# Sums of squares by TensorE for the second norm, and five gate/up tiles with two products ahead of the main loop

## The chip, the cores and the metric

The kernel runs on one NeuronCore of a Trainium2 chip. The metric is the device time of one execution in microseconds; the time of a kernel is the median of its runs. The engines are TensorE (PE in the profile, with its weight loads as PEld), VectorE (DVE), ScalarE (ACT), GpSimd (POOL), and SyncE (SP), which here only issues transfers.

## What is computed

Two layers of an encoder trunk over 1,040 positions (16 learned ones and 1,024 of the input), with 1,024 features. Each layer is a mixer and a feed-forward part, each behind an RMSNorm and added to the residual; the change lies at the second norm of each layer:

```python
def rmsnorm(x, w):
    xf = x.astype(jnp.float32)
    y = xf * lax.rsqrt(jnp.mean(xf * xf, axis=-1, keepdims=True) + RMS_EPS)
    return (y * w.astype(jnp.float32)).astype(x.dtype)

def swiglu(h, w_gate_up, w_down):
    gate, up = jnp.split(h @ w_gate_up.astype(h.dtype), 2, axis=-1)
    return (jax.nn.silu(gate) * up) @ w_down.astype(h.dtype)
...
    for l in range(DEPTH):
        h = h + hybrid_mixer(rmsnorm(h, norm1_w[l]), ..., w_out[l])
        h = h + swiglu(rmsnorm(h, norm2_w[l]), w_gate_up[l], w_down[l])
```

The mixer is a delta-rule head group beside a gated convolution, joined by one output projection `w_out`. Everything is float32; the feed-forward has 2,816 inner features, so 22 tiles of 128.

## The kernel before

**Layout.** Features lie on the 128 partitions, positions along the row: the residual `hr` is eight tiles of 128 x 1040. A sum of squares over features is therefore a sum over eight tiles and then over partitions. In the second layer the feed-forward leaves out the 16 learned positions (`o0 = 16`), so its rows have 1,024 columns.

**Products.** A float32 product is made of three passes in the fast fp32r form: both operands are split into a high part (`hi`, by a copy on ACT) and the rest (`lo`, by a subtraction on POOL or DVE), and PE adds hi*hi, hi*lo and lo*hi in one bank (`dense`, L145 to L172; `prod`, L1055). The splitting of a weight block of 128 x 512 is `wsplit` (L129, L130) for the projections and `w_op` (L1042, L1043) for gate and up.

**The feed-forward's scheme.** Gate and up together are one product, done by a Strassen-Winograd scheme with seven products per tile in place of eight. Its left operands are the weight blocks A11, A12, A22 and sums S1 to S4 of blocks; its right operands are parts and sums of the scaled residual: B11, B21, B22 and T1 to T4, each 128 x 4 x `NB` as a hi and a lo part. `NB` is half a row: 520 columns in layer 0, 512 in layer 1. The halves are made of quarters of the row: half 0 is the two middle quarters, half 1 the two outer ones (`half`, L932). In layer 0 a product is made in two pieces of 260 columns (`NJ` = 2), in layer 1 in one of 512. B11 and B21 need half 0 alone.

**Order of the work around the change.**

1. `out_part(z, m)` (L941) adds to half `z` of residual tile `m` the part of the output projection that comes from the delta-rule heads: `dense` with DVE's `add_h` (L905) as evacuation, in two column chunks, then the square on ACT, the running sum of squares in `ss` on DVE or POOL, and a store of the tile to `hd`. It runs over `m` for z = 0, then for z = 1.
2. Between the parts, DVE and ACT build the T operands: `t_split_w` (L177 and L176, a scaled split), scalings of the other half in place (L1001, which must wait until the store to `hd` has read the tile), sums (`t_sum`, L977), and `t_split` (L964 on ACT, L965 on DVE).
3. The early tiles: for the first `NE` = 4 of 22 tiles the two products that need only half 0, A11*B11 and A12*B21, are done here, ahead of the main loop (L1083 to L1098). Their results wait in the rows `u` and `g`; ACT copies them out (L1095, L1098).
4. `finish_bc` (L200) closes the sum: four matmuls with a block of ones, each on a quarter of the columns and into 32 partitions of its own of one bank, so that all positions lie as 4 x 32 partitions by 260 (256) columns; then the root on ACT, the reciprocal on DVE, a store of 4 rows and a broadcast back into `ss`:

```python
        for j in range(4 if sums else 0):
            mm(ps[32 * j:32 * j + 32, 0:e], ones[:, 0:32], ss[:, n0 + e * j:n0 + e * j + e], start=True, stop=True, skip_group_check=True)
        r = c4k("r")[:, 0:e]
        act(out=r, in_=ps[:, 0:e], func=AF.Sqrt, scale=1.0 / D, bias=cols["eps"])
        nc.vector.reciprocal(out=r, in_=r)
```

5. The main loop over 22 tiles (L1256): weight loads on SP's queue, the sums S1 to S4 on DVE (L1266, L1267, L1270, L1271), their splits (`w_op`), five products for the early tiles and seven for the others, with DVE adding the products together (L1289, L1300, L1303, L1307, L1316). Some additions stand between two products that share a bank, so that the second product waits for them. Then gate and up are multiplied by the reciprocal root `ss` (L1330 on POOL, L1331 on DVE), SiLU, the product of both (L1333), and the store to `ad`.
6. Among the main loop's tiles stand eight sums S1 of the down projection's weights (L1146), loaded by SP into `c` buffers.

At the first norm of the kernel the sums of squares are already made by PE: eight sets of four fp32 matmuls of 260 columns (`first_sums`, L252).

**What sets the order.** The program is written in the order of one thread; a scheduler (Tile, with a timeline of its own and the priorities set by `at_prio`) decides where each instruction stands in the queue of its engine. Each queue is then worked off in order. Banks of PSUM come from rings: `acc` has three, `f` and `b` two, `a` one (L69); `pbank` (L1048) deals them out for gate and up. Full rows called `c` (`c4k`, L65) are a ring of two that serves the squares, `r`, the `u` of the last early tile and later the S1 sums. The weight tiles `whi`/`wlo` have three buffers, `raw` two, and the row buffers `ck2` five.

Of the kernel before, what the change touches and what calls it, by code (L numbers as in the profile page):

```python
# [7 lines left out]
F32 = mybir.dt.float32  # L8
F32R = mybir.dt.float32r
BF16 = mybir.dt.bfloat16  # L10
AF = mybir.ActivationFunctionType
# [4 lines left out]
KT = 8  # L16
# [26 lines left out]
def trunk(ctx: ExitStack, tc: tile.TileContext, xT, w_in, w_ba, w_out, w_gu, w_dn,  # L43
# [15 lines left out]
    def row(tag, dt=F32, bufs=1):  # L59
        return sb.tile([128, L], dt, tag=tag, bufs=bufs, name=nm(tag))  # L60
# [4 lines left out]
    def c4k(tag="c"):  # L65
        return sb.tile([128, L], F32, tag="c", bufs=2, name=nm(tag))

    def bank(tag):
        return psp.tile([128, 512], F32, tag=tag, bufs={"acc": 3, "a": 1, "f": 2, "b": 2}[tag], name=nm("p" + tag))  # L69
# [62 lines left out]
    def wload(src, nk):  # L132

        res = []
        step = min(nk, WK)
        for k0 in range(0, nk, step):
            kk = min(step, nk - k0)
            hi = wp.tile([128, WK, 128], F32R, tag="whi", name=nm("whi"))
            lo = wp.tile([128, WK, 128], F32R, tag="wlo", name=nm("wlo"))
            wsplit(src[:, k0:k0 + kk, :], hi[:, 0:kk, :], lo[:, 0:kk, :])  # L140
            for k in range(kk):
                res.append((hi[:, k, :], lo[:, k, :]))
        return res

    def dense(ws, xs, chunks, evac, pool=None):  # L145

        for (n0, n1) in chunks:
            n = n1 - n0
            ps = (pool or pacc)()
            K = len(xs)  # L150
            here = tc.cur_priority
            if mmp[0] is not None:
                at_prio(mmp[0])
            for k in range(K):
                (wh, wl), (xh, xl) = ws[k], xs[k]
                mm(ps[:, :n], wh, xh[:, n0:n1], start=(k == 0), stop=False)  # L156
                mm(ps[:, :n], wh, xl[:, n0:n1], start=False, stop=False)  # L157
                mm(ps[:, :n], wl, xh[:, n0:n1], start=False, stop=(k == K - 1))  # L158
            if mmp[0] is not None:
                mmp[0] = tc.cur_priority  # L160
                at_prio(here)
            here = tc.cur_priority
            if evp[0] is not None:
                at_prio(evp[0])
            evac(ps[:, :n], n0, n1)
            if evp[0] is not None:
                evp[0] = tc.cur_priority
                at_prio(here)
            for q in (jobs, jobs2, jobs3):
                f = q.pop(0) if q else None  # L170
                if f is not None:
                    f()  # L172
# [27 lines left out]
    def finish_bc(ss, n0, n1, dst, ps=None):  # L200

        e = (n1 - n0) // 4
        sums = ps is None
        ps = bank("a") if sums else ps
# [5 lines that stand above are left out]
        dma(dst[:, 0:e], r.rearrange("(a b) c -> a b c", b=32)[:, 0, :])  # L210
        if 4 * e == L:
            dma(ss[:, n0:n1], dst.rearrange("a e -> (a e)").partition_broadcast(128))
        else:
            dma(ss[:, n0:n1].rearrange("p (a e) -> p a e", a=4), dst[:, 0:e].partition_broadcast(128))
# [64 lines left out]
    for l in range(DEPTH):  # L279
# [623 lines left out]
        def add_h(m, then=None):  # L903
            def f(ps, n0, n1):
                tt(out=hr[m][:, n0:n1], in0=ps, in1=hr[m][:, n0:n1], op=ALU.add)  # L905
                if then is not None:
                    then(n0, n1)
            return f
# [23 lines left out]
        def half(ap, z):  # L932

            v = ap.rearrange("p (g e) -> p g e", g=4) if len(ap.shape) == 2 else ap.rearrange("p k (g e) -> p k g e", g=4)
            s = slice(1, 3) if z == 0 else slice(0, 4, 3)
            return v[:, s, :] if len(ap.shape) == 2 else v[:, :, s, :]

        at_prio(base + 3000000)
        ss = row("rstd")

        def out_part(z, m):  # L941
            dense(wload(w_out[l, m, :, 0:4, :], 4), os_, hcut[z], add_h(m), pwide)

            v, sv = half(hr[m][:, o0:L], z), half(ss[:, o0:L], z)
            if m == 0:
                act(out=sv, in_=v, func=AF.Square)
            else:
                sq = c4k("sq")[:, 0:NB].rearrange("p (g e) -> p g e", g=2)
                act(out=sq, in_=v, func=AF.Square)
                (ptt if z == 1 and m % 2 == 0 else tt)(out=sv, in0=sv, in1=sq, op=ALU.add)  # L950
            for (n0, n1) in hcut[z]:
                dma(hd[m][:, n0:n1], hr[m][:, n0:n1])

# [36 lines left out]
        for m in range(KT + 2):  # L990
            if m < KT:
                out_part(1, m)
            if m == 0:
                t_split_w(T["B21"], 7, 0)
            k = m - 2
            if k < 0:
                continue
            if k < 4:
                if k == 0:
                    T["T1"] = t_tile(Y[0][2])  # L1000
                ts(out=hx(k, 1), in0=hx(k, 1), scalar1=pcol(P_N2 + k), scalar2=None, op0=ALU.mult)  # L1001
                t_sum(k, 0, hx(k, 0), npar[:, k:k + 1], hx(k, 1), ALU.add)
                if k % 2:
                    t_split(T["T1"], X0, 0, k - 1)
            else:
                c = pcol(P_N2 + k)
                if k == 4:
                    T["B22"] = t_tile(Y[0][1])
                t_split_w(T["B22"], k, 1)
                t_sum(k - 4, 1, hx(k, 1), c, hx(k - 4, 1))  # L1010
                t_sum(k, 1, hx(k, 1), c, hx(k - 4, 0))
                t_sum(k, 0, hx(k, 0), c, hx(k, 1))
# [67 lines left out]
            return loc(ps, 0)  # L1080


        NE = 4  # L1083
        early = {}
        for f in range(NE):
            A11, A12 = raw4("raw"), raw4("raw")
            dma(A11, w_gu[l, f, 0, :, 0:4, :])
            dma(A12, w_gu[l, f, 0, :, 4:8, :])
            w1, w2 = w_op(A11, True), w_op(A12, True)
            g, u = (row(Y[1], F32, 3), row(X[1], F32, 3)) if f < 3 else (row(Y[1] + "f"), c4k())  # L1090
            early[f] = g, u
            ab = [pbank() for j in range(NJ)]
            for j in range(NJ):
                prod(ab[j], w1, T["B11"], j, True)
                act(out=part(u, 0, j), in_=pin(ab[j]), func=AF.Copy)  # L1095
            for j in range(NJ):
                prod(ab[j], w2, T["B21"], j, False)
                act(out=part(g, 0, j), in_=pin(ab[j]), func=AF.Copy)  # L1098

        finish_bc(ss, o0, L, rsd[0])  # L1100

# [399 lines left out]
```

## Time and profile before

| | |
|---|---|
| time, median of 3 runs | 2607.66 us (2607.26 to 2610.53) |
| the profiled execution's own time | 2614.81 us |
| its span, first to last instruction | 2612.7 us |
| mean granted TensorE clock | 0.984 |
| busy: PE, DVE, ACT, POOL | 96%, 63%, 40%, 42% |

The page and the trace are of one execution, the profiled one. A line such as `L252 PE MATMUL pb<-sq,ones x64` names the line of the kernel, the engine, the operation, the tile written, those read, and how often; forms stand as partitions x columns. A line of the timeline starts with the start in us and the duration; the bracket at its end is the idle time of the engine before it and what ended it. Starts of matmuls follow each other faster than their durations, since they are pipelined. One fp32 matmul of the program is two instructions in the profile.

### The profile page before, as it was taken

What the parts mean: (1) busy time and instruction counts of PE and PEld (TensorE: products, weight loads), DVE (VectorE), ACT (ScalarE), POOL (GpSimd) and SP (SyncE); (2) the same over time, 40 slices, a digit from 0 to 9 for tenths busy, and PEclk for the clock granted to TensorE, in tenths of its full rate; (3) what the DMA queues carried; (4) which work ended last, traced back from release to release, by engine and by line L of the source; (5) the groups of instructions that cost most, each with busy time, mean ns of one, the idle gap of its engine ahead of it and who ended that gap; (6) DMA issues with size and microseconds to landing.
All of it is one profiled execution on the core that took longest, in us unless ns stands there. A gap on an engine that the chain in (4) does not pass through costs nothing.

```text
span 2612.7 us, 45153 instructions
## 1 busy us (share of the span) xinstructions
PE 2508.1 (96%) x17442; PEld 2294.1 (88%) x17442; DVE 1654.4 (63%) x2481; ACT 1045.9 (40%) x1933; POOL 1105.0 (42%) x838
## 2 busy tenths in 40 slices
PE   8999999999999999989999989999989999998997
PEld 6989999898899999989999978998967778886876
DVE  4688433648766666667656874236688777668656
ACT  5664322435233333434445633324452333333444
POOL 2141311225666666645321203122367667665552
PEclk9999999999999999989999999999999999999998
DMA  3458264524422222763324581545333222248431
GB/s 126 135 185 268 90 215 148 176 80 125 135 91 99 94 74 74 252 198 111 97 86 136 186 283 63 182 159 197 116 121 129 94 102 85 79 141 273 133 108 65
DMA packets 213571, 360.03 MB, mean 138 GB/s; under 512 B 25268, under 2 KB 87676, under 8 KB 213356
## 3 DMA queue, kind: packets, MB, share of 16 engines
q1 hardware_dynamic: 180684, 310.69, 36.1%
q10 hardware_dynamic: 30496, 42.09, 5.1%
q0 software_dynamic: 2176, 4.36, 0.6%
q8 instruction: 137, 2.24, 0.4%
q14 instruction: 78, 0.64, 0.1%
HBM read 266.60 MB, written 90.46 MB: 137 GB/s over the span
## 4 chain that ended last, share of the span: by engine, by line
PE 54%; DVE 9%; DMA 4%; issue 3%; POOL 2%; ACT 1%; POOLq 0%; ACTq 0%; DVEq 0%; SPq 0%
PE pacc L156 5%; PE pacc L158 5%; PE pacc L157 5%; PE pacc L1060 3%; PE pacc L1062 3%; PE pacc L1061 3%; PE pb L1060 2%; PE pf L1060 2%; PE pb L1062 2%; PE pb L1061 2%; PE pf L1062 2%; PE pf L1061 2%; PE pacc L1400 1%; PE pacc L1402 1%; PE pacc L1401 1%
## 5 line engine op out<-in xcount | busy, mean ns | idle before, releaser
L130 POOL TENSOR_TENSOR wlo<-raw,whi 128x512 fp32r<-128x512 f32 x132 | 177.0, 1342 | 788.3 <-ACT whi L129 639.4
L156 PE MATMUL pacc<-a,whi 128*128 128x346 f32 (+1 forms) x808 | 265.5, 332 | 10.2 <-ACT whi L129 8.3
L158 PE MATMUL pacc<-a,wlo 128*128 128x346 f32 (+1 forms) x808 | 265.1, 330 | 0.4 <-DVE wlo L130 0.4
L156 PE MATMUL pacc<-b,whi 128*128 128x346 f32 (+2 forms) x672 | 234.8, 350 | 0.0
L158 PE MATMUL pacc<-b,wlo 128*128 128x346 f32 (+2 forms) x672 | 233.2, 348 | 0.0
L157 PE MATMUL pacc<-a,whi 128*128 128x346 f32 (+1 forms) x688 | 227.5, 331 | 2.7 <-DVE a L900 2.5
L129 ACT ACTIVATE whi<-raw 128x512 fp32r<-128x512 f32 x168 | 105.3, 629 | 244.6 <-PE pacc L157 169.3
L157 PE MATMUL pacc<-b,whi 128*128 128x346 f32 (+2 forms) x580 | 200.5, 347 | 0.5 <-DVE b L900 0.5
L156 PEld LDWEIGHTS pacc<-a,whi 128*128 128x128 f32 x808 | 154.5, 192 | 14.5 <-ACT whi L129 10.1
L1043 POOL TENSOR_TENSOR wlo<-rw,whi 128x512 fp32r<-128x512 f32 x92 | 134.8, 1467 | 71.7 <-ACT whi L1042 70.0
L158 PEld LDWEIGHTS pacc<-a,wlo 128*128 128x128 f32 x808 | 154.5, 191 | 2.1 <-issue 0.8
L157 PEld LDWEIGHTS pacc<-a,whi 128*128 128x128 f32 x688 | 132.2, 192 | 7.1 <-issue 2.9
L156 PEld LDWEIGHTS pacc<-b,whi 128*128 128x128 f32 x672 | 127.3, 190 | 11.0 <-issue 3.1
L158 PEld LDWEIGHTS pacc<-b,wlo 128*128 128x128 f32 x672 | 127.3, 190 | 9.2 <-issue 0.8
L1043 POOL TENSOR_TENSOR a<-rw,a 128x512 fp32r<-128x512 f32 x64 | 105.6, 1651 | 69.5 <-ACT a L1042 69.3
L1043 POOL TENSOR_TENSOR b<-rw,b 128x512 fp32r<-128x512 f32 x64 | 92.0, 1439 | 82.3 <-ACT b L1042 49.5
L157 PEld LDWEIGHTS pacc<-b,whi 128*128 128x128 f32 x580 | 109.9, 190 | 7.8 <-DVE b L900 1.0
L1042 ACT ACTIVATE whi<-rw 128x512 fp32r<-128x512 f32 x92 | 57.8, 630 | 146.5 <-DVE rw L1270 84.8
L1266 DVE TENSOR_TENSOR rw<-rw,rw 128x512 f32<-128x512 f32 x44 | 67.4, 1532 | 49.9 <-POOL wlo L1043 34.6
L1271 DVE TENSOR_TENSOR rw<-raw,rw 128x512 f32<-128x512 f32 x44 | 97.4, 2214 | 1.2
L1043 POOL TENSOR_TENSOR wlo<-raw,whi 128x512 fp32r<-128x512 f32 x50 | 76.6, 1533 | 36.5 <-ACT whi L1042 27.9
L1042 ACT ACTIVATE b<-rw 128x512 fp32r<-128x512 f32 x64 | 40.2, 630 | 119.8 <-PE pacc L1061 32.3
(970 smaller groups left out, 8420.2 us busy)
## 6 DMA issues: line engine op xcount, KB each, us to landing
raw<-in_w_in SPq DMA_DIRECT2D x112, 256.0 KB
raw<-in_w_gu SPq DMA_DIRECT2D x104, 256.0 KB
rw<-in_w_gu SPq DMA_DIRECT2D x88, 256.0 KB
rec<-aqd SPq DMA_DIRECT2D x62, 256.0 KB
rec<-vkd SPq DMA_DIRECT2D x61, 256.0 KB
rw<-in_w_dn SPq DMA_DIRECT2D x70, 192.0 KB
raw<-in_w_out SPq DMA_DIRECT2D x48, 256.0 KB
b<-ad SPq DMA_DIRECT2D x45, 260.0 KB
```

The costliest lines, as they stand in the source:

```text
L129: act(out=hi, in_=raw[:, 0:kk, :], func=AF.Copy)
L130: (tt if lov[0] else ptt)(out=lo, in0=raw[:, 0:kk, :], in1=hi.bitcast(F32), op=ALU.subtract)
L156: mm(ps[:, :n], wh, xh[:, n0:n1], start=(k == 0), stop=False)
L157: mm(ps[:, :n], wh, xl[:, n0:n1], start=False, stop=False)
L158: mm(ps[:, :n], wl, xh[:, n0:n1], start=False, stop=(k == K - 1))
L1042: act(out=hi, in_=src, func=AF.Copy)
L1043: ptt(out=lo, in0=src, in1=hi.bitcast(F32), op=ALU.subtract)
L1060: mm(ps[:, :CW], w[0][:, k, :], th[:, cs], start=first and k == 0, stop=False, skip_group_check=True)
L1061: mm(ps[:, :CW], w[0][:, k, :], tl[:, cs], start=False, stop=False, skip_group_check=True)
L1062: mm(ps[:, :CW], w[1][:, k, :], th[:, cs], start=False, stop=stop and k == nk - 1, skip_group_check=True)
L1266: tt(out=s1t, in0=A21, in1=A22, op=ALU.add)
L1271: tt(out=A21, in0=A11, in1=A21, op=ALU.subtract)
```

## The change

The running sum in `ss` goes. In its place each square of 128 x 520 (512) is summed over the partitions by PE: four fp32 matmuls with 32 columns of ones, on quarters of 130 (128) columns, into four strips of 32 partitions of the one bank `a`, which adds up over all eight tiles. Half 0 lies in the left, half 1 in the right part of the bank's first 260 (256) columns. The matmuls of one square are issued behind the next part's `dense` (`sq_sums`). The square of the first tile goes to a `c` buffer like the others. `sq_finish` does the root and the reciprocal, once for both halves, a store of 4 rows, and four broadcast loads that put each strip back to its quarter of the row; it stands in the loop of the second half after its last tile, so ahead of the early tiles. `finish_bc` there goes. The early tiles become five; the fifth keeps its gate in a row of its own and its up in a `c` buffer.

```diff
+        QB = NB // 4
+        sqs = []
+        sps = bank("a")
+
+        def sq_sums():
+            while sqs:
+                sq, z, m = sqs.pop()
+                for j in range(4):
+                    mm(sps[32 * j:32 * j + 32, QB * z:QB * z + QB], ones[:, 0:32], sq[:, QB * j:QB * j + QB], start=(m == 0), stop=(m == KT - 1), skip_group_check=True)
+
+        def sq_finish(dst):
+            sq_sums()
+            r = c4k("r")[:, 0:2 * QB]
+            act(out=r, in_=sps[:, 0:2 * QB], func=AF.Sqrt, scale=1.0 / D, bias=cols["eps"])
+            nc.vector.reciprocal(out=r, in_=r)
+            dma(dst[:, 0:2 * QB], r.rearrange("(a b) c -> a b c", b=32)[:, 0, :])
+            for z in range(2):
+                for i in range(2):
+
+                    q = (1 + i, 3 * i)[z]
+                    dma(ss[:, cut[q]:cut[q + 1]].rearrange("p (a e) -> p a e", a=2), dst[2 * i:2 * i + 2, QB * z:QB * z + QB].partition_broadcast(128))
+
         def out_part(z, m):
             dense(wload(w_out[l, m, :, 0:4, :], 4), os_, hcut[z], add_h(m), pwide)
-
-            v, sv = half(hr[m][:, o0:L], z), half(ss[:, o0:L], z)
-            if m == 0:
-                act(out=sv, in_=v, func=AF.Square)
-            else:
-                sq = c4k("sq")[:, 0:NB].rearrange("p (g e) -> p g e", g=2)
-                act(out=sq, in_=v, func=AF.Square)
-                (ptt if z == 1 and m % 2 == 0 else tt)(out=sv, in0=sv, in1=sq, op=ALU.add)
+            sq_sums()
+
+            sq = c4k("sq")[:, 0:NB]
+            act(out=sq.rearrange("p (g e) -> p g e", g=2), in_=half(hr[m][:, o0:L], z), func=AF.Square)
+            sqs.append((sq, z, m))
             for (n0, n1) in hcut[z]:
                 dma(hd[m][:, n0:n1], hr[m][:, n0:n1])
...
             k = m - 2
+            if m == KT:
+                sq_finish(rsd[0])
...
-        NE = 4
+        NE = 5
         early = {}
         for f in range(NE):
             A11, A12 = raw4("raw"), raw4("raw")
             dma(A11, w_gu[l, f, 0, :, 0:4, :])
             dma(A12, w_gu[l, f, 0, :, 4:8, :])
             w1, w2 = w_op(A11, True), w_op(A12, True)
-            g, u = (row(Y[1], F32, 3), row(X[1], F32, 3)) if f < 3 else (row(Y[1] + "f"), c4k())
+            g, u = (row(Y[1], F32, 3), row(X[1], F32, 3)) if f < 3 else (row((Y, X)[f % 2 == 0][1] + "f"), c4k())
...
-        finish_bc(ss, o0, L, rsd[0])
```

## The prediction

> **What bounds the kernel now.** I read the page's busy shares first, then a table of stretches around the two places of the change, then TensorE's own waits there. A layer's second norm lies between the output projection and the feed-forward's main loop: about 570 to 740 us in layer 0, 1860 to 2020 us in layer 1.
>
> ```profile
> PE 2508.1 (96%) x17442; PEld 2294.1 (88%) x17442; DVE 1654.4 (63%) x2481; ACT 1045.9 (40%) x1933; POOL 1105.0 (42%) x838
> ...
> 590.00:600.00 10.00, 10.00 (x86) 10.00 (x85) 6.92 (x13) 4.70 (x8) 4.87 (x4) 1.00 0.62 175
> 610.00:620.00 10.00, 6.36 (x49) 5.76 (x48) 10.00 (x14) 5.76 (x9) 5.91 (x4) 0.97 0.33 96
> 620.00:630.00 10.00, 8.65 (x53) 8.66 (x54) 10.00 (x12) 6.42 (x12) 4.81 (x5) 0.69 0.39 118
> 1910.00:1920.00 10.00, 8.87 (x31) 6.44 (x31) 10.00 (x11) 5.97 (x10) 6.89 (x4) 0.85 0.39 125
> 1980.00:2000.00 20.00, 15.87 (x60) 11.95 (x59) 17.17 (x16) 4.92 (x8) 16.38 (x9) 0.91 0.41 134
> 2150.00:2200.00 50.00, 50.00 (x217) 40.52 (x216) 36.26 (x32) 15.96 (x26) 32.91 (x20) 1.00 0.28 101
> ```
>
> A stretch's columns are its length, then busy us and count of PE, weight loads, DVE, ACT and POOL, then the granted TensorE clock. PE is 96% busy: matrix work added in a stretch like 590 to 600 lengthens the run one for one, while an instruction taken from DVE or POOL there is worth nothing. From 610 to 630 it is the other way round: DVE has no idle time, PE has 5 us of it and runs part of the rest at a reduced clock. What PE waits for there, by engine, awaited instruction, us in total, times, longest, first in layer 0 (594 to 742 us), then in layer 1 (1896 to 2020 us):
>
> ```profile
> PE pacc L1060 <- DVE a L905: 2.5, 1, 2.5
> PE pa L1060 <- DVE b L1303: 2.1, 1, 2.1
> PE pacc L1060 <- DVE a L1289: 1.8, 2, 1.3
> PE pf L1060 <- DVE a L905: 1.4, 1, 1.4
> PE pf L1060 <- DVE c L1307: 1.4, 1, 1.4
> PE pb L1060 <- DVE a L1307: 1.3, 1, 1.3
> PE pacc L1060 <- DVE a L1307: 1.3, 1, 1.3
> PE pb L1060 <- ACT whi L1042: 1.0, 1, 1.0
> ...
> PE pf L1060 <- DVE b L905: 2.7, 1, 2.7
> PE pa L1060 <- DVE a L1303: 2.4, 1, 2.4
> PE pf L1060 <- DVE b L1307: 2.0, 1, 2.0
> PE pa L206 <- DVE rstd L950: 1.4, 1, 1.4
> PE pa L1060 <- DVE c L1289: 1.2, 1, 1.2
> PE pb L1062 <- POOL wlo L1043: 1.2, 1, 1.2
> PE pf L1060 <- ACT b L1095: 1.0, 1, 1.0
> PE pb L1060 <- ACT b L1042: 0.9, 1, 0.9
> PE pf L156 <- DVE b L905: 0.7, 1, 0.7
> ```
>
> The waits fall in two groups. L905 is DVE's add of an output chunk to the residual: PE wants the bank back and DVE is behind. L1289, L1303 and L1307 are DVE's additions of products in the main loop's first tiles. The change can win only these waits and the slow clock; everything it adds to PE outside them is paid.
>
> **The price of the sums.** The first norm already forms its sums as the change does, with four quarters of 260 columns. One such set in its surroundings:
>
> ```profile
> 32.63 0.32 PE L157 MATMUL pf<-a3f,whi 128*128 128x348 f32 x1
> 32.79 0.32 PE L158 MATMUL pf<-a,wlo 128*128 128x348 f32 x1
> 33.03 0.65 PE L252 MATMUL pb<-sq,ones 128*32 128x260 f32 x8
> 33.61 0.43 PE L156 MATMUL pacc<-a,whi 128*128 128x346 f32 x1
> 33.88 0.33 PE L157 MATMUL pacc<-a,whi 128*128 128x346 f32 x1
> ...
> L206 PE MATMUL pa<-rstd,ones x24: 376/383/407, 647.0 to 1923.0; 128*32 128x260 f32 x16, 128*32 128x256 f32 x8
> L808 PE MATMUL pf<-vv,P x128: 270/275/275, 358.3 to 1797.7; 128*128 128x128 f32 x128
> ```
>
> Starts without the set are 0.16 us apart (32.63, 32.79), so two matmuls after 32.79 would start at 33.11; the second starts at 33.88. The set costs 0.77 us: 0.08 before it, 0.58 for itself, 0.11 behind it. The new sets have 130 (layer 1: 128) columns. An fp32 instruction takes 383 ns with 260 and 275 ns with 128 columns, 108 ns less; the four quarters run beside each other (8 instructions in 0.65 us), and each quarter is two instructions in a row, so 0.22 us go: 0.55 us a set. Bounds: 0.39 if all of it shrinks with the columns, 0.77 if nothing does. The edges of 0.08 and 0.11 at 260 columns are what decides for 0.55. The Trainium skill (TensorEngine Tiling (Array Packing), Key Properties) says that changing the tiling mode drains the array. That speaks against this change: by it each of the 16 sets pays two drains whatever its width, and without them its sum would be some 3 us a layer lower.
>
> Each layer has 16 sets instead of the one of L206: 16 x 0.55 - 0.77 = 8.0 us, both layers +16.1 us (bounds +10.9 and +23.1). Eight sets follow products of the first half, where PE has no gap, and are paid in full; the others fall where it has gaps.
>
> **What DVE and POOL lose.**
>
> ```profile
> L950 DVE TENSOR_TENSOR rstd<-rstd,sq x22: 687/701/1757, 573.8 to 1920.8; 128x520 f32<-128x520 f32 x11, 128x512 f32<-128x512 f32 x11
> L950 POOL TENSOR_TENSOR rstd<-rstd,sq x6: 1299/1742/1771, 601.8 to 1913.8; 128x520 f32<-128x520 f32 x3, 128x512 f32<-128x512 f32 x3
> ...
> 651.98 1.77 DVE L209 RECIPROCAL r<-r 128x260 f32<-128x260 f32 x1
> ...
> L949 ACT ACTIVATE sq<-a x14: 622/638/642, 573.1 to 621.7; 128x520 f32<-128x520 f32 x14
> ...
> 638.06 3.47 DVE L965 TENSOR_TENSOR a<-a,a 128x1040 fp32r<-128x1040 f32 x2
> ...
> 646.45 0.28 PE L1062 MATMUL pacc<-b,wlo 128*128 128x260 f32 x1
> 646.57 0.28 PE L1060 MATMUL pacc<-b,whi 128*128 128x260 f32 x1
> ```
>
> Of a layer's 14 adds, DVE's seven in the first half are worth nothing (PE is full). Its four in the second half, 4 x 0.70 = 2.8 us or more, and POOL's three of 1.74, leave a full DVE; as PE's second half also grows by eight sets (4.4 us), DVE should no longer be late with L905. I count those waits as gone: 2.5 + 1.4 in layer 0, 2.7 + 0.7 in layer 1, there also the 1.4 for L950 itself and the 1.0 for ACT's copy (L1095) queued behind squares; half of ACT's 1.0 (L1042) in layer 0. The slow clock goes with its cause. At full clock, starts of 260 columns are 0.12 us apart (646.45, 646.57): the 49 + 53 matmuls from 610 to 630 need 12.2 us, but PE was busy 15.0, so 2.8. In layer 1 a matmul takes 50.00 / 217 = 0.23 us: 31 need 7.1 of 8.87, so 1.7. The Trainium skill (TensorE: Matmul & The Clock Gate, section Why this matters for your kernels) asks only that gaps stay below about 3 us. By that, no wait here slows the clock, closing them brings nothing beside the waits, and the sum would be 4.5 us higher, 2614.9; the trace shows 0.69 after a longest wait of 2.5, so the trace decides. Together 6.7 + 0.5 and 7.5: -14.7 us (between -7, if a third of the waits and the clock stay, and -16).
>
> The reciprocal stays 260 wide; it moves from the main loop's start to before the last T splits, where it holds the DVE queue for 1.77 us. The last split ends at 638.06 + 3.47 = 641.5; PE then still has early tiles to run until 647, later with a fifth tile: no one waits. The root, the small store and the broadcast loads (four for one, on SP's queue among the weight loads) now stand ahead of the fourth early tile, long before the first multiplication by rstd: I cost them at nothing.
>
> A new wait: PE stands in order at each set until ACT has squared a row that DVE has added. Behind it are all projections. In the changed order, sets of the second half stand 27 to 37 matmuls behind the last product they depend on, at least 27 x 0.12 = 3.2 us; the square takes 0.64, so DVE may be 2.5 us late. I put 0.5 us for both layers (0 to 6).
>
> **The fifth early tile.** Its two products are the same 48 matmuls, 5.8 us, done earlier; PE's total does not change. The extra loads of A11 and A12 (both are loaded again in the loop) meet queues that are not full. They fill no wait that isn't already gone: PE would be busy to the main loop anyway. But tile 4 then has five products instead of seven in the loop, and such tiles show the waits: layer 0's waits for L1289, L1303 and L1307 sum to 7.9 us, layer 1's for DVE and ACT in the loop to 6.5. About 1.4 us a tile, so +2.8. On the other side the ring of two "c" buffers now gives the second one to tile 4's u, and the sums S1 of the down weights (L1146) need both: in the changed order all eight stand behind tile 3. In layer 0 such a sum held DVE for a DMA and PE with it:
>
> ```profile
> 682.60 1.67 DVE L1146 TENSOR_TENSOR b<-S 128x384 f32<-128x384 f32 x1 [2.70 <-DMA S<-in_w_dn]
> ...
> 685.20 0.39 PE L1060 MATMUL pa<-P,a 128*128 128x260 f32 x1 [2.11 <-DVE b L1303]
> ```
>
> This 2.1 and layer 1's 2.0 for L1307 leave tiles 0 to 3 (-4.1); half returns in tiles 4 and 5 (+2). Sum for the main loop +0.8 us (from -8 to +8).
>
> **Sum.** 16.1 - 14.7 + 0.5 + 0.8 = +2.7 us. The profiled execution took 2614.81 us, span 2612.7, so 2617.5; it stands 7.15 above the median of 2607.66, to which I carry the difference: **2610.4 us**. A measurement of this kernel can tell about 0.2% (5.2 us) from no change, so this is no change.
>
> **Rivals.**
> - *The loop's waits close too.* With the S1 sums out of tiles 0 to 3 and weights further ahead, half of 7.9 + 6.5 goes, tile 4 costs nothing, and the clock of 0.91 (60 x 0.23 = 13.8 of 15.87: 2.1) recovers: 16.1 - 14.7 - 7.2 - 2.1 = -8, about 2600 us. For it: the row at 682.60. Against: tiles of five products have few others to run while an addition is awaited, and there is one more. Chance 0.22.
> - *Slower: S1 sums crowd into tiles 4 and 5.* Eight sums in two tiles, each after its own DMA into one pair of buffers; if half of them pass 2.1 us to PE as at 685.20, that is 4 x 2.1 = 8.4 a layer, less the 4.1 saved for both: 16.1 - 14.7 + 2.8 + 16.8 - 4.1 = +17 at worst, +8 with half of it: 2616 us. It decides if DVE, with sums, takes longer than PE's seven products. Chance 0.15.
> - *Slower: PE waits for squares.* If DVE is over 2.5 us late, waits for L905 turn into waits at sets, the clock stays low: 16.1 and no more than 5 us won, +11, 2619 us. Chance 0.10.
> - *The sums are paid and nothing closes*, since another engine's wait takes each freed place: +16, 2624 us. Chance 0.05.
>
> My own case has 0.48; the set at 0.39 or 0.77 moves it by 5 or 7 us, so a sixth of it lies beyond 0.2%, more above. That gives faster 0.24, same 0.41, slower 0.35. The range from 2600 (first rival) to 2621 leaves out the last rival and the tails; the likeliest case alone has 2605 to 2617.
>
> **What would show it.** Right: sets of about 0.4 us on the page's scale with 0.1 us lost at either side; no wait for L905 after 600 us and a clock of 1.0 from 610 to 630; PE at the main loop some 7 us later than now (8.0 - 7.2 + 5.8), with 48 matmuls fewer ahead of it; waits for additions around tile 4. Wrong: PE waiting for the square at sets; long DVE stops at the S1 sums with PE behind them; sets above 0.7 us; or main-loop waits under 5 us a layer.

## The result and the profile after

| | before | after |
|---|---|---|
| time, median | 2609.10 us (2607.26 to 2613.18, 4 runs) | 2629.39 us (2624.70 to 2631.94, 4 runs) |
| ratio to before, 95% interval | 1 | 1.0067 [1.0053, 1.0082], that is +17.5 us [13.8, 21.4] |
| profiled execution, span | 2612.7 us | 2627.8 us |
| its granted clock | 0.984 | 0.985 |

The change is slower; 2610.4 us had been forecast, between 2600 and 2621. The two medians lie 20.3 us apart; the 17.5 of the ratio is used below, and both lie inside its interval. Ratios are used below as so many us of 2608; an interval of a ratio is some 2.5 to 4 us to either side, so a difference of two ratios is known to some 4 to 6 us.

**Where the 15.1 us between the two profiled spans lie.** The same events in both traces: at the first L905 the changed kernel is already 3.5 us late, though everything up to there is the same program (a difference of executions); from there to tile 7's product (L1333, L1353 after) it loses 12.0 us in layer 0 and 7.2 in layer 1; the way from there to layer 1's first L905 gives 1.7 back and the end of layer 1 5.9 (there the execution of before stood at a bank and a slow clock, see e4). So the change's own place, first L905 to tile 7, costs 19.2 us in the profile. That stretch as windows, layer 0 and layer 1, first before, then after; columns are the length and then PE's busy us and count:

```profile
516.90:802.00 285.10, 270.36 (x2108) 262.78 (x2107) 192.84 (x277) 103.99 (x191) 148.47 (x95) 0.99 0.33 105
1806.80:2093.60 286.80, 272.30 (x1401) 227.31 (x1401) 214.43 (x262) 108.56 (x206) 157.93 (x98) 0.99 0.36 118
```

```profile
520.40:817.50 297.10, 279.26 (x2227) 266.68 (x2227) 187.49 (x266) 103.14 (x191) 146.47 (x92) 0.99 0.32 102
1820.60:2114.60 294.00, 282.47 (x1532) 233.00 (x1532) 196.49 (x254) 108.72 (x207) 147.84 (x96) 0.98 0.37 117
```

PE is busy 270.36 + 272.30 = 542.7 us before and 561.7 after: +19.1. Its idle time is 14.7 + 14.5 = 29.2 us before and 17.8 + 11.5 = 29.4 after. The sets are paid in full, and not one microsecond of waiting has gone on balance, although DVE lost 23 and POOL 12 us of work. The prediction had 10.2 us of waiting leave, and 4.5 us of slow clock, which would show as busy time.

**The sets** cost what was predicted. One of them in the changed kernel's timeline:

```profile
586.33 0.28 PE L158 MATMUL pacc<-o,wlo 128*128 128x260 f32 x1
586.54 0.43 PE L950 MATMUL pa<-sq,ones 128*32 128x130 f32 x8
586.90 0.39 PE L156 MATMUL pacc<-o,whi 128*128 128x260 f32 x1
587.13 0.28 PE L157 MATMUL pacc<-o,whi 128*128 128x260 f32 x1
```

Two matmuls after 586.33 would start 0.24 us later, at 586.57; the second starts at 587.13: 0.56 us a set, 0.55 predicted.

**The waits that were to go have gone, and others stand in their place.** Windows of the changed kernel around the second half, then PE's waits, in layer 0 (598 to 790 us) and in layer 1 (1900 to 2110):

```profile
610.00:620.00 10.00, 9.45 (x91) 8.30 (x90) 8.65 (x15) 5.82 (x9) 2.59 (x2) 1.00 0.50 144
620.00:630.00 10.00, 9.10 (x83) 8.14 (x82) 10.00 (x13) 5.72 (x9) 5.33 (x3) 1.00 0.38 122
```

```profile
PE pb L1082 <- DVE b3f L1323: 4.2, 2, 2.8
PE pf L1082 <- DVE a3f L1323: 3.0, 1, 3.0
PE pacc L1082 <- ACT a L1117: 1.9, 1, 1.9
...
PE pa L1082 <- DVE c L1336: 1.4, 1, 1.4
PE pacc L1082 <- DVE c L1327: 1.4, 1, 1.4
...
PE pa L950 <- ACT sq L969: 1.0, 3, 0.5
...
PE pa L1082 <- DVE b L1327: 3.6, 1, 3.6
PE pacc L1082 <- ACT whi L1064: 2.8, 1, 2.8
PE pacc L1084 <- POOL wlo L1065: 2.5, 2, 1.9
PE pa L950 <- ACT sq L969: 0.9, 3, 0.4
```

L905 is in neither list, the stretch from 610 to 630 has PE at 9.45 and 9.10 of 10 at full clock (6.36 and 8.65 before, at 0.97 and 0.69), and the squares hold PE for 1.0 and 0.9 us only. In their place stand two kinds of wait. The first two rows alone are 7.2 us. L1323, L1327 and L1336 (L1303, L1307 and L1316 before) are additions of products; those in these rows lie in tiles 4 to 6. L1117, L1064 and L1065 (L1095, L1042 and L1043 before) are the copies of the early tiles and the weight splits. Summed over all of PE's waits in these stretches before and after, 8.7 us went (7.3 for L905, 1.4 for L950), and 9.0 came: 1.9 for squares, 3.9 more for copies and splits (from 1.8 to 2.6 in layer 0, from 3.3 to 6.4 in layer 1) and 3.2 more for additions (from 8.6 to 13.7 in layer 0, but from 6.3 down to 4.4 in layer 1).

**Tiles 4 to 6 in layer 0.** DVE's stops at the S1 sums of the down weights (L1166; L1146 before) and PE behind them, from the two timelines of the changed kernel:

```profile
750.10 1.63 DVE L1166 TENSOR_TENSOR b<-S 128x384 f32<-128x384 f32 x1 [1.10 <-DMA S<-in_w_dn]
...
753.88 0.41 DVE L1323 TENSOR_TENSOR b3f<-pb,b3f 128x260 f32<-128x260 f32 x1
...
761.41 0.56 DVE L1166 TENSOR_TENSOR b<-S 128x384 f32<-128x384 f32 x1 [4.76 <-DMA S<-in_w_dn]
...
762.34 0.43 DVE L1323 TENSOR_TENSOR b3f<-pb,b3f 128x260 f32<-128x260 f32 x1
```

```profile
754.35 0.39 PE L1082 MATMUL pb<-P,a 128*128 128x260 f32 x1 [2.80 <-DVE b3f L1323]
762.82 0.39 PE L1082 MATMUL pb<-P,a 128*128 128x260 f32 x1 [1.38 <-DVE b3f L1323]
```

All eight sums stand between 741 and 775 us (between 677 and 730 in the kernel before). DVE stops 4.76 us for one load, and the addition that frees PE's bank is queued behind. The wait tables put 10.7 us of DVE's time in layer 0 and 9.2 in layer 1 down to these loads; in the kernel before it was 5.9 and 9.4, so in layer 1 DVE stops no longer than it did.

### The profile page after: what moved, and what is told of

Same layout as the page of the kernel before. It is cut to its first block, busy times and chain, and to the rows that moved or that the text cites. A ratio compares the mean times of both kernels' runs of the same rounds, so it can differ in the third digit from the quotient of the medians.

```text
span 2627.8 us, 45584 instructions
## 1 busy us (share of the span) xinstructions
PE 2521.0 (96%) x17682; PEld 2297.4 (87%) x17682; DVE 1628.8 (62%) x2459; ACT 1044.6 (40%) x1933; POOL 1095.0 (42%) x832
## 4 chain that ended last, share of the span: by engine, by line
PE 69%; DVE 12%; DMA 8%; issue 4%; ACT 3%; POOL 3%; ACTq 0%; SPq 0%; POOLq 0%; DVEq 0%
PE pacc L156 7%; PE pacc L158 7%; PE pacc L157 7%; PE pacc L1082 3%; PE pacc L1084 3%; PE pacc L1083 3%; PE pf L1082 2%; PE pb L1082 2%; PE pf L1083 2%; PE pf L1084 2%; PE pb L1084 2%; PE pb L1083 2%; PE pacc L1420 2%; PE pacc L1422 2%; PE pacc L1421 2%
## 5 line engine op out<-in xcount | busy, mean ns | idle before, releaser
L130 POOL TENSOR_TENSOR wlo<-raw,whi 128x512 fp32r<-128x512 f32 x132 | 175.1, 1328 | 801.2 <-ACT whi L129 666.0
L156 PE MATMUL pacc<-a,whi 128*128 128x346 f32 (+1 forms) x808 | 264.7, 331 | 10.2 <-ACT whi L129 8.2
L1065 POOL TENSOR_TENSOR wlo<-raw,whi 128x512 fp32r<-128x512 f32 x86 | 131.5, 1530 | 88.6 <-ACT whi L1064 78.5
L156 PEld LDWEIGHTS pacc<-a,whi 128*128 128x128 f32 x808 | 153.8, 191 | 14.8 <-ACT whi L129 9.6
L1065 POOL TENSOR_TENSOR a<-rw,a 128x512 fp32r<-128x512 f32 x81 | 130.0, 1608 | 72.2 <-ACT a L1064 66.1
L1065 POOL TENSOR_TENSOR b<-rw,b 128x512 fp32r<-128x512 f32 x81 | 114.3, 1415 | 91.3 <-ACT b L1064 61.5
L1065 POOL TENSOR_TENSOR wlo<-rw,whi 128x512 fp32r<-128x512 f32 x58 | 87.4, 1510 | 69.8 <-ACT whi L1064 61.0
L1064 ACT ACTIVATE b<-rw 128x512 fp32r<-128x512 f32 x81 | 50.7, 629 | 132.7 <-PE pf L1083 29.3
L1064 ACT ACTIVATE a<-rw 128x512 fp32r<-128x512 f32 x81 | 50.9, 631 | 111.8 <-PE pacc L1083 50.3
L1291 DVE TENSOR_TENSOR rw<-raw,rw 128x512 f32<-128x512 f32 x44 | 89.3, 2030 | 1.1
```

The costliest lines, as they stand in the source:

```text
L130: (tt if lov[0] else ptt)(out=lo, in0=raw[:, 0:kk, :], in1=hi.bitcast(F32), op=ALU.subtract)
L1064: act(out=hi, in_=src, func=AF.Copy)
L1065: ptt(out=lo, in0=src, in1=hi.bitcast(F32), op=ALU.subtract)
L1291: tt(out=A21, in0=A11, in1=A21, op=ALU.subtract)
```

## Experiments

Two theories were set against each other. **A**: the sets cost their 0.56 us, the waits for L905 do close, and the loss comes from the S1 sums, which crowd into the tiles behind the early ones. **B**: closing those waits is worth little, because the work behind them is late for reasons of its own, so that the sets are simply added. In the later expectations, A and B are the two answers to that run's own question.

### The two parts alone

**e1, sums by PE with four early tiles.** The change with

```diff
-        NE = 5
+        NE = 4
```

> Sums of squares by TensorE as in the change, but four early tiles as before. Theory A (the loss is the fifth early tile, which lets all eight S1 sums of the down weights run behind tile 3, where they crowd tiles 4 and 5): 16 sets at 0.56 us for the one of before are 8.2 us a layer, against waits for the residual adds and the slow clock of some 7 us won; the S1 sums stand among tiles 0 to 3 as before. So +1 to +5 us on before (2610 to 2614 on a median of 2609). Theory B (the sums are paid in full, and the freed time is taken by other waits ahead of the main loop): +14 to +17 us, about the whole loss.

Measured 2617.55 us, 1.0031 [1.0022, 1.0040], +8.1 us: between the two.

**e2, five early tiles with the sums as before.** The ring of two `c` buffers allows it only with `finish_bc` ahead of the early tiles:

```diff
+        finish_bc(ss, o0, L, rsd[0])
-        NE = 4
+        NE = 5
...
-        finish_bc(ss, o0, L, rsd[0])
```

> Sums as before (adds on VectorE and GpSimd, four closing matmuls), five early tiles; the closing of the sum stands ahead of the early tiles, since with five of them its buffer would otherwise wait for a tile that needs it. Theory A: the crowd in tiles 4 to 6 of layer 0 comes without the new sums, so +7 to +12 us. Theory B: the fifth tile fills idle time while VectorE is behind, 0 to -6 us.

Measured 2616.29 us, 1.0027 [1.0014, 1.0041], +7.0 us: the lower edge of theory A. Within their intervals the parts add up (8.1 + 7.0 = 15.1 of 17.5), and each loses by itself.

### The S1 sums held back

A scheduling dependency puts each of the eight S1 sums behind the last multiplication of the tile where the program has it (tiles 8 to 15), in place of the early place that the scheduler chose:

```diff
-        def s_sum(which, n, room=None):
+        def s_sum(which, n, room=None, prev=None):
...
-                tt(out=S, in0=a_load(r, 1, 0, n), in1=a_load(o, 1, 1, n), op=ALU.add)
+                after(tt(out=S, in0=a_load(r, 1, 0, n), in1=a_load(o, 1, 1, n), op=ALU.add), prev)
...
-            s_under(f)
+            s_under(f, last_mult)
```

**e3, in the changed kernel.**

> The changed kernel, with each of the eight S1 sums held behind the last product of its own tile (tiles 8 to 15), one sum a tile. Theory A: the long stops of VectorE for the loads of the S1 sums leave tiles 4 to 6, TensorE's waits of 2.8, 3.0, 1.4 and 1.1 us for VectorE's additions there go, 7 to 10 us less than the change, about 2620. Theory B: no more than 2 us less.

Measured 2612.45 us, 1.0014 [1.0005, 1.0024]: 13.8 us below the change, more than theory A's 7 to 10. From PE's waits of this kernel in the same stretch of layer 0 (598 to 790 us), the longest and those of the lines named:

```profile
PE pacc L1082 <- ACT a L1117: 1.9, 1, 1.9
PE pa L1082 <- DVE a L1309: 1.6, 1, 1.6
PE pa L1082 <- ACT whi L1064: 1.6, 1, 1.6
PE pa L1082 <- DVE c L1336: 1.4, 1, 1.4
PE pf L1082 <- DVE b L1323: 1.0, 1, 1.0
...
PE pacc L1082 <- DVE a L1327: 0.4, 1, 0.4
```

The 4.2, 3.0 and 1.0 at L1323 are down to one wait of 1.0, the 1.4 and 1.1 at L1327 to 0.6 in all; one wait of 1.6 for a weight split (L1064) is new. That holding these sums back is worth about 14 us to the changed kernel is shown; what else the scheduler ordered anew in doing so was not separated from it. But is this the change's doing?

**e6, in the kernel before.**

> The kernel before, with each of the eight S1 sums of the down weights held behind the last multiplication of its own tile (tiles 8 to 15). Theory A, S1 sums that come early stop VectorE for their loads and cost the kernel before too (2.1 us in layer 0, 2.0 in layer 1 in its trace): about -4 us, 2604 to 2606. Theory B, holding them back gains only where five early tiles and the sums by TensorE had crowded them: 0, within 2 us.

Measured 2599.82 us, 0.9968 [0.9956, 0.9981], -8.3 us: more than either theory had, and the fastest complete kernel here. The sums cost the kernel before 8.3 us already. In the change their price is 13.8, so 5.5 us more; the prediction had it fall by 2.1. The waits for L1307 of 1.4 and 1.3 us in layer 0, which the prediction left in place, are gone here with the 2.1 for L1303.

**e7, with the sums by PE and four early tiles; e14, with five early tiles and the sums as before.**

> Sums of squares by TensorE, four early tiles, and the S1 sums held behind their own tiles. Theory A, the +8 us of the sums alone were half S1 sums (7.0 us of waits for additions in layer 0's loop): 2612 to 2614, +4 on before. Theory B, the +8 us are the sets' 16 less the few waits that closed, and the new waits for the weight splits in layer 1: no change on the sums alone, 2616 to 2618.5.

> Additions of squares by VectorE and POOL as before, the norm's end ahead of the early tiles, five early tiles, S1 sums held behind their own tiles. Theory A, the fifth tile is free once the sums are held (with sums by TensorE the step from four to five gave -1.3 us): 2597 to 2602, level with the kernel before with held sums. Theory B, the norm's end ahead of the early tiles puts VectorE's late additions on the path of TensorE (4.1 us of waits for L1288 and 2.1 for the reciprocal's buffer in the run without held sums): 2605 to 2610.

e7: 2613.75 us, 1.0018 [1.0005, 1.0031], as its theory A had it. e14: 2603.75 us, 0.9982 [0.9966, 0.9999], between its two. All eight corners, in us from the kernel before:

| | S1 sums where the scheduler put them | held | difference |
|---|---|---|---|
| before | 0 | -8.3 | 8.3 |
| sums by PE (e1, e7) | +8.1 | +4.7 | 3.4 |
| five early tiles (e2, e14) | +7.0 | -4.7 | 11.7 |
| both, the change (after, e3) | +17.5 | +3.7 | 13.8 |

One difference here is known to some 3 to 6 us, so the step from 8.3 to 13.8 doesn't stand clear of the noise by itself. The means of both ways of summing do: holding the sums is worth 5.9 us at four early tiles (8.3 and 3.4) and 12.8 at five (11.7 and 13.8). With the S1 sums held, the fifth tile costs -1.0 us (beside sums by PE) to +3.6 (without): near nothing. Without that, it costs 7.0 and 9.4: most of the fifth tile's loss is the crowd of S1 sums. The sums by PE cost 13.0 us at four tiles and 8.4 at five with S1 held. So theory A explains the fifth tile and not the sums.

### What the sums cost

Windows from the first L905 to tile 7, layer 0 and layer 1, of the kernel before with held S1 sums (e6), then of the one with sums by PE (e7):

```profile
518.80:798.90 280.10, 268.70 (x2108) 261.80 (x2107) 185.66 (x269) 104.04 (x191) 149.83 (x95) 0.99 0.29 97
1801.60:2081.60 280.00, 270.30 (x1401) 226.25 (x1401) 207.50 (x254) 108.79 (x206) 157.31 (x98) 0.99 0.33 112
```

```profile
517.80:805.00 287.20, 278.20 (x2227) 266.44 (x2227) 179.22 (x258) 104.00 (x191) 146.93 (x92) 0.99 0.29 94
1807.70:2093.80 286.10, 279.26 (x1528) 231.29 (x1528) 188.68 (x243) 108.76 (x206) 147.12 (x95) 0.99 0.33 108
```

Busy +9.5 and +9.0 us; idle 11.4 to 9.0 and 9.7 to 6.8. The sets are paid, 5.3 us of waiting go.

**e5, every set issued twice** (on e1):

```diff
-                for j in range(4):
-                    mm(..., start=(m == 0), stop=(m == KT - 1), skip_group_check=True)
+                for i in range(2):
+                    for j in range(4):
+                        mm(..., start=(m == 0 and i == 0), stop=(m == KT - 1 and i == 1), skip_group_check=True)
...
-            act(out=r, in_=sps[:, 0:2 * QB], func=AF.Sqrt, scale=1.0 / D, bias=cols["eps"])
+            act(out=r, in_=sps[:, 0:2 * QB], func=AF.Sqrt, scale=0.5 / D, bias=cols["eps"])
```

> Sums of squares by TensorE, four early tiles, and every set of four quarters issued twice (the root's scale is halved, so the result stays). 32 more sets in both layers. Theory A, sets are paid in full at the 0.56 us read from the trace: 32 x 0.56 = +17.9 us on the kernel with the sums alone (2617.5), so about 2635, +26 on before. Theory B, the sets lie partly in gaps, and what the kernel with the sums alone loses comes from elsewhere: +9 us or less on it, 2626 or below.

Measured 2621.59 us, 1.0055 [1.0043, 1.0068]: +6.3 us on e1 for 32 sets, 0.20 each (the intervals leave 0.07 to 0.33). By its number that is theory B; its reason was wrong, as the timeline of a doubled set shows:

```profile
591.09 0.28 PE L156 MATMUL pf<-o,whi 128*128 128x260 f32 x1
591.29 0.65 PE L951 MATMUL pa<-sq,ones 128*32 128x130 f32 x16
...
592.10 0.29 PE L158 MATMUL pf<-o,wlo 128*128 128x260 f32 x1
```

The second matmul after the set starts 592.10 - 591.09 - 0.24 = 0.77 us late, against 0.56 for one set: the second eight instructions cost 0.21, and 32 x 0.21 = 6.7. So 0.35 of the 0.56 does not grow with the number of instructions in the set: it is the price of going over to the sets and back. The trace agrees with the drain that the prediction took from the Trainium skill (TensorEngine Tiling (Array Packing), Key Properties). But a set also changes from fp32r to float32 matmuls, and no run here separates the two.

**e13, the relief without the sets** (on e7): neither DVE and POOL add squares nor does PE sum them; only the last row's set is issued, so the norm is of one row in eight.

```diff
-                for j in range(4):
+                for j in range(4 if m == KT - 1 else 0):
-                    mm(..., start=(m == 0), stop=(m == KT - 1), skip_group_check=True)
+                    mm(..., start=True, stop=True, skip_group_check=True)
```

> The kernel with the sums by TensorE and held S1 sums (2613.75), with the sets of the first seven rows of each half left out (only the last row's set is issued, so the norm is of one row in eight): neither VectorE and POOL add squares nor does TensorE sum them. Against the kernel before with held S1 sums (2599.8) it prices the relief alone. Theory A, the relief is worth what the prediction credited, about 10 us of waits and some slow clock: 2585 to 2591. Theory B, other waits take the freed places: 2596 to 2601, and the sets (28 x 0.56 = 15.7 us) are paid with nothing against them. In both the difference to 2613.75 should be near 15.7.

Measured 2595.81 us, 0.9951 [0.9937, 0.9965], 0.2 us below what theory B had. The 28 sets cost 17.5 us (0.62 each; the intervals leave 0.4 to 0.8). Taking all adds of squares from DVE and POOL is worth 4.4 us against e6, and the intervals of the two overlap, so it may be nothing. Its windows from the first L905 to tile 7, layer 0 and layer 1, to be held against those of e6 above, and its PE waits in layer 0:

```profile
515.60:795.80 280.20, 269.44 (x2115) 261.79 (x2115) 179.06 (x259) 103.83 (x191) 147.54 (x92) 0.99 0.29 97
1798.00:2073.40 275.40, 270.62 (x1416) 228.41 (x1415) 195.09 (x244) 109.17 (x206) 151.69 (x95) 0.99 0.33 113
```

```profile
PE pb L1082 <- ACT whi L1064: 2.3, 1, 2.3
PE pacc L1082 <- ACT a L1064: 2.2, 2, 1.8
PE pacc L1082 <- DVE a L1309: 2.1, 2, 1.7
PE pa L1082 <- ACT whi L1064: 1.7, 1, 1.7
```

In the profiled executions nothing is won in layer 0 (280.20 us against 280.10): there are six us of waits for weight splits on ACT, where e6 has 1.7. When PE is no longer held at L905, it arrives at the early tiles and the first loop tiles before their weights are split. Layer 1 wins 4.6 us (275.40 against 280.00); there the waits for splits hardly grow, from 3.4 to 3.9 us.

### Why the weights are late

In the changed kernel, ACT's copies that free PE's banks stand behind a split that waits for a load. First a row of SP's timeline in the changed kernel, then ACT's:

```profile
635.87 0.33 SPq L1110 DMA_DIRECT2D raw<-in_w_gu  x1
640.97 0.53 SPq L957 DMA_DIRECT2D rsd<-r  x1
```

```profile
638.49 0.63 ACT L1064 ACTIVATE whi<-raw 128x512 fp32r<-128x512 f32 x1 [2.42 <-DMA raw<-in_w_gu]
...
639.29 0.38 ACT L1117 ACTIVATE a<-pacc 128x260 f32<-128x260 f32 x1
```

SP's own waits there had `SPq L957 <- DVE r L956` with 4.7 us: the small store waits for the reciprocal, with later early loads behind it. The prediction had costed that place at nothing, so I suspected it. The rows themselves speak against that for this wait: the load at 635.87, for which ACT waits until 638.49, stands ahead of the store.

**e9 to e12, the store held behind the early tiles' last copy:** in the changed kernel (e9), in e3 (e10), in e7 (e11) and in e12's kernel below.

```diff
-            dma(dst[:, 0:2 * QB], r.rearrange("(a b) c -> a b c", b=32)[:, 0, :])
+            return r
+
+        def sq_send(r, dst, prev):
+            after(dma(dst[:, 0:2 * QB], r.rearrange("(a b) c -> a b c", b=32)[:, 0, :]), prev)
...
+        sq_send(rr, rsd[0], last_copy)
```

> The changed kernel, with the small store of the reciprocal held until tile 3's last product has been copied, so that it and the four broadcast loads stand behind the early tiles' weight loads on SP's queue. In the changed kernel SP stands 4.7 us at that store for the reciprocal, and ACT then stands 5.7 us at three splits for the loads behind it, with the copies that free TensorE's banks queued after the splits. Theory A, this queue place passes 1.9 us of wait and a slow clock to TensorE in layer 0 and the same order of it in layer 1: 3 to 8 us less than the changed kernel, 2621 to 2626. Theory B, the early loads are late for another reason (their buffers are freed by POOL's splits): no change, within 2 us of 2629.

> The changed kernel with both: the store held behind the early tiles' loads, and each S1 sum held behind its own tile. Theory A, the two losses are separate and add: 3 to 8 us less than the changed kernel with held sums alone (2612.4), 2604 to 2609. Theory B, held sums already took all that SP's place costs: 2611 to 2614.

> Sums of squares by TensorE, four early tiles, S1 sums held behind their tiles, and the store held behind the early tiles' loads, where the kernel before had it. Theory A, SP's place is what the sums cost beside their sets: 3 to 8 us less than with held sums alone (2613.75), 2606 to 2610; what is then left above the kernel before with held sums (2599.8) is the sets' 16 less the waits for additions. Theory B: no change, 2612 to 2615.

| | with the store held | without |
|---|---|---|
| the change | e9: 2629.94 us, 1.0085 [1.0072, 1.0098] | 1.0067 [1.0053, 1.0082] |
| and S1 held | e10: 2610.25, 1.0010 [1.0000, 1.0020] | e3: 1.0014 [1.0005, 1.0024] |
| sums by PE, S1 held | e11: 2617.37, 1.0035 [1.0023, 1.0047] | e7: 1.0018 [1.0005, 1.0031] |

It helps nowhere: my suspicion fell. e9 is its theory B, e10 lies between its two, e11 above both. PE's wait for the copy is still there in e11, and SP's order shows why:

```profile
627.60 0.37 SPq L1112 DMA_DIRECT2D raw<-in_w_gu  x1
632.65 0.33 SPq L1113 DMA_DIRECT2D raw<-in_w_gu  x1
...
636.53 0.39 PE L1085 MATMUL pacc<-a,whi 128*128 128x260 f32 x1 [1.92 <-ACT a L1120]
```

No store stands between 627.60 and 632.65. The second load waits for POOL's split of an earlier weight block to free one of the two `raw` buffers, ACT for that load, PE for ACT. The loads of the early tiles pass through two buffers, one split after another. The rows show that this chain held PE at this place; how much of the whole loss it makes stays open, since a third `raw` buffer was not tried.

**e8 and e12, half of the sums.** DVE adds the first half's squares as before (PE is full there, DVE has room) and one set closes them; the second half keeps its eight sets: 9 sets a layer. Four early tiles, S1 sums held; e12 also holds the store.

```diff
-            sqs.append((sq, z, m))
...
+                if z == 0:
+                    tt(out=s0, in0=s0, in1=sq, op=ALU.add)
+                else:
+                    sqs.append((sq, z, m))
+            if z == 0 and m == KT - 1:
+                sqs.append((s0, 0, None))
```

> First half's squares added by VectorE as before (where TensorE has no gap and VectorE is free), then one set for them; second half's eight rows by one set each; four early tiles; S1 sums held behind their own tiles. 9 sets a layer instead of 16: 14 x 0.56 = 7.8 us less than with all sets. Theory A, a first-half set costs its 0.56 in full: about 2605, 3 to 4 us below before. Theory B, VectorE with the first half's seven additions is late again and the waits for the additions (L905) come back: within 3 us of the kernel with all sets and held sums.

> The first half's squares added by VectorE, 9 sets a layer instead of 16, S1 sums held, and the store held behind the early tiles' loads. Theory A: 3 to 8 us less than without the held store (2603.2), 2595 to 2600, so level with or below the kernel before with held sums (2599.8). Theory B: no change, 2601 to 2605, and the sums by TensorE never pay.

e8: 2603.22 us, 0.9984 [0.9975, 0.9993]: 8.9 us below e7 for 14 sets less (14 x 0.56 = 7.8), as theory A had it, and still not below e6. e12: 2610.33 us, 1.0013 [1.0004, 1.0022], 7.6 us above e8, the contrary of what was expected. In e12 the broadcast is issued at 657.7 us in place of 635.6, and POOL's first multiplication by it moves from 663.7 to 668.0. But in both kernels the trace has POOL wait there for an addition on DVE (4.81 us in e12) and not for the broadcast; what makes the 7.6 us stays open.

### The end of layer 1

**e4, a bank.** Before's profile had 5.9 us more than after's at the end. In e4 the kernel before deals the banks of layer 1 one further:

```diff
-        bn = [0]
+        bn = [1 if last else 0]
```

> The kernel before, with the bank sequence of the second layer's feed-forward shifted by one, as the fifth early tile shifts it; nothing else. In the trace of before, TensorE waits 2.9 us for bank a (released by a VectorE add, L1406) in the second layer's down projection, and the clock drops behind it; the changed kernel has no such wait. If the bank sequence is the reason: -4 to -6 us on before. If the wait only moves: 0.

Measured 2608.72 us, 0.9997 [0.9987, 1.0007]. The wait of 2.9 us for bank `a` goes from the trace, and the median doesn't change. The 5.9 us are no gain of the change: from tile 7 of layer 1 to the end, the profiled executions of these kernels spread from 513 to 522 us, without order.

## Why the prediction was wrong

- **The price of a set, 0.55 us: right** (0.56 in the trace). Busy time rose by 19.1 us: 32 x 0.56 less two of 0.77 is 16.4, and up to 1.7 of the rest is the one slow step more that is told below.
- **The waits for L905 and L950 went, as predicted, and that for L1095 in layer 1 fell from 1.0 to 0.3 us (one of 1.9 for the same line came in layer 0). The credit for them, -14.7 us with the slow clock, is the step that failed.** I took a wait that disappears for time that is gained, and named what is late next only for the square and for additions. In the changed kernel PE waits 3.9 us more for the copies and weight splits (loads through two `raw` buffers, splits on ACT and POOL), 3.2 more for additions and 1.9 for squares, and its idle time stays. With the sets taken out (e13) the whole relief is worth 4.4 us, with the sets in, idle time falls by 5.3 (e7 against e6). So some 10 of the 14.8 us by which the forecast was too low lie here. That the weight chain is next is read from waits; no run has lifted it.
- **The slow clock, 4.5 of those 14.7: it did not go, it moved.** The stretch has four slow steps before and five after; see below.
- **The new wait for squares, 0.5 us: 1.9.** Small.
- **The main loop, +0.8 (from -8 to +8): wrong in its parts.** "Leave tiles 0 to 3 (-4.1); half returns in tiles 4 and 5 (+2)" is the second step that failed: the price of the S1 sums did not fall by 2.1 us but rose, from 8.3 to 13.8 (5.9 to 12.8 in the mean of both ways of summing). I had read their price before as 4.1, from the two waits with a load right ahead of them, and missed that the same sums push back additions that the table puts down to DVE: in e6 two more such waits, for L1307, went with them. The fifth tile's five products, +2.8, measured -1.0 to +3.6.
- **The rivals.** The crowd in tiles 4 and 5 (chance 0.15, "+17 at worst") happened, at less than its worst: in layer 0 the waits at 754.35 and 762.82 are what it described. "Sums paid and nothing closes" (0.05, 2624) is nearest to the idle time of 29.2 and 29.4. They came together; I had priced each alone, so the range ended at 2621. PE hardly waits for squares; the loop's waits did not close.
- **The store and the broadcast on SP's queue, nothing:** SP does stand 4.7 us there, and no kernel gained from moving it.

## What to carry to other kernels

A wait is worth what the next-latest input leaves of it. Before crediting it, ask for each wait that goes where PE will stand instead, with its own loads and splits included; the test is to take the relief alone (here e13: 4.4 us of 14.7, and perhaps nothing) before paying for it. And look for instructions that an in-order queue meets too early for their data: holding eight additions behind later work was worth 8.3 us by itself, while the change around which all this was built cost 17.5.

## What the hardware showed

The slow clock comes in whole steps. Windows of the kernel before, then of the changed one, in pairs: 3.4 us ahead of a slow period, and the period; the third column is PE's busy time, and the granted clock stands third from the end:

```profile
616.00:619.40 3.40, 1.80 (x13) 1.38 (x11) 3.40 (x5) 3.17 (x6) 2.86 (x2) 1.00 0.33 99
619.40:626.20 6.80, 4.85 (x22) 4.86 (x23) 6.80 (x8) 3.40 (x8) 4.08 (x3) 0.50 0.50 142
```

```profile
636.80:640.20 3.40, 1.51 (x13) 1.30 (x12) 3.40 (x3) 1.46 (x4) 1.69 (x2) 1.00 0.23 77
640.20:643.60 3.40, 3.40 (x18) 3.40 (x17) 3.02 (x4) 2.05 (x3) 0.33 (x1) 0.50 0.20 66
...
1944.10:1947.50 3.40, 0.60 (x3) 0.22 (x2) 3.40 (x4) 3.17 (x5) 0.19 (x1) 1.00 0.00 1
1947.50:1954.30 6.80, 4.95 (x12) 3.36 (x12) 1.53 (x2) 1.22 (x3) 3.88 (x2) 0.50 0.62 157
```

In these rows the clock is 1.00 or 0.50, it is slow for 3.4 or 6.8 us, and each slow period follows a stretch of 3.4 us in which PE was busy about half or less (1.80, 1.51, 0.60). That is no full rule: in e4 the clock fell at 533.0 us after 3.41 us in which PE was busy throughout. The prediction's 0.69 of a 10 us window was two such steps; the wait of 2.5 us that it set beside them ended at 621.35, inside the slow period, and of layer 0's waits in its table the longest that had ended before the fall was 1.4 us. One step costs up to 1.7 us (half of 3.4), so a cluster of waits costs more than its sum, and it moves with the cluster. Before, the stretch from the first L905 to tile 7 has two steps at 619, one at 1910 and one at 1995; in the changed kernel it has one each at 640, 780 and 2067 and two at 1947. The Trainium skill (TensorE: Matmul & The Clock Gate, What's actually happening) has half speed after an idle window of about 3.4 us. The trace agrees with the two speeds and the step, but the window needn't be idle: 1.80 us of work in 3.40 was not enough.
